# Gate and up projections in pairs: another buffer for half a weight set of the first pair, and another order of loads

## The chip, the cores and the metric

The kernel runs on one NeuronCore of a Trainium2 chip. Its engines are TensorE (matrix products; the profile's PE for matmuls, PEld for the weight loads beside them), VectorE (DVE), ScalarE (ACT), GpSimd (POOL) and SyncE (SP); each works through its own instructions in its own order. SP and POOL also issue the DMA transfers, each on a queue of its own, and both queues share 16 DMA engines. The metric is device time of one execution in microseconds (us). The profile is one execution of the program, taken by the hardware profiler.

## The reference, cut to what matters

One layer of a hybrid encoder on a sequence of 512 tokens of 1024 channels in float32. Three token mixers in parallel come first and are merged and projected; then follows the part that the change touches, a gated feed-forward network of width 2816:

```python
h2 = rms_norm(x, norm_ffn[l])
act = jax.nn.silu(jnp.einsum('bsd,df->bsf', h2, w_ffn_gate[l])) * jnp.einsum('bsd,df->bsf', h2, w_ffn_up[l])
x = x + jnp.einsum('bsf,fd->bsd', act, w_ffn_down[l])
```

## The kernel before

**Precision.** A float32 operand is split in two float32r parts: ScalarE rounds it to a high part, VectorE subtracts this from the operand and gives the low part (`split_a`, L1546 to 1554). A product is then three matmuls (high by high, high by low, low by high). The split weights lie in tags `whi` and `wlo` with 3 buffers each, so that splits run at most about two sets ahead of TensorE.

**The columns of the feed-forward network.** The 2816 columns are 11 chunks of 256. The first two (`NDIRECT`) are computed directly: `chan_chunk` for gate and up, `direct_act` for the activation (L1705 to 1721). The next six are taken as three pairs of chunks, u = 0, 1, 2 (`NTOK`, `seven_tok`, L1633), and the last three one by one, u = 3, 4, 5 (`seven`, L1587). Both of the latter compute gate and up together, by a scheme of seven products instead of eight: the operands are a 2 x 2 matrix of weight blocks (row: gate or up; column: first or second half of the 1024 input channels) and the normed input in blocks B. The seven weight operands of a pair, in the order of use (`ORDER`, L175), are

- 11, 12: blocks as loaded (gate, first and second half of the channels);
- S2 = 11 + 21 + 22 with the sign convention of the loaded blocks, S1 = 21 + 22, S3 = 11 + 21, S4 = S2 + 12;
- 22: as loaded (up, second half).

For a pair (u < 3) each weight set comes in two halves i = 0, 1 of 512 KB (128 partitions x 1024 values), written here 12_0, 12_1 and so on; S3_0, say, is the first half of S3. Each half is 12 matmuls of 512 columns (L1677). Products 11, S2 and S3 go to PSUM tile `ps_yh`, 12 to `ps_xl`, S1 and S4 to `ps_xh`, 22 to `ps_yl`.

**How the sets are made.** `make_a` (L1515) goes through `steps` (pair, set, half) some sets ahead of TensorE, and at each step loads, adds and splits what the step needs:

- `load_a(u)` (L1491) loads the sets that are built by accumulation. For pair 0: 21 (then 22 is added onto it by an accumulating DMA from POOL, giving S1) and 11 under the name S3 (then 21 is added by POOL, giving S3). For pairs 1 and 2: 11 and 21 (22 added by POOL, L1503). The loads are issued by SP (L1501). All of them lie in `corner` buffers.
- `load_raw(u, nm)` (L1505) loads 11, 12 and 22 by SP (L1509) into tag `raw` of pool `wp` (3 buffers). One half is an exception: 12_1 of pair 0 lies in a `g4` buffer.
- `make_s2` (L1511, VectorE at L1513) adds 21 and 11 to S2 in a `g4` buffer; L1542 adds 12 to it after S2 has been split, giving S4. For pairs 1 and 2, L1540 adds 21 onto 11 by a POOL DMA, giving S3, after 11 has been split.

**Buffers.** `corner` is a pool of 8 buffers of 4 KB a partition (L1270). Ahead of pair 0 they hold the 8 normed blocks and their differences (`hn`, `hnT`; L1444 and L1456); `split_b` (L1449) splits these for the seven products, and each buffer is free once all readers of its block are done. `g4` is a pool of 27 such buffers (`GBUFS`).

**When pair 1's loads are written.** L1519 calls `load_a` one pair ahead. While make_a is at 11, 12 or S2 of pair 0 only `load_a(0)` has been called; at S1 of pair 0 `load_a(1)` is. The order in which the instructions of an engine are finally issued is set by a planner (the Tile scheduler) from priorities, buffers and its own model of the times, and not by the order of the code alone; `tc.issue_after(ins)` adds an edge behind one instruction of the same engine. `make_a(3)` at L1709 is the first call, beside the direct chunk 1; it reaches 12_0 of pair 0.

Of the kernel before, what the change touches and what calls it, by code (L numbers as in the profile page):

```python
# [65 lines left out]
def layer_kernel(ctx: ExitStack, tc: tile.TileContext, x, xt, vecs, w_in, w_qkv7, w_gate7, w_pool, w_rg, w_ig,  # L66
                 w_branch, w_br7, w_out, w_fg, w_fu, w_fgu7, w_fgl7, w_fd, w_fd7, out):
    nc = tc.nc
# [51 lines left out]
    def two2(ap):  # L120
        if ap.shape[-1] == H:
            return ap.rearrange("p w (a b) -> p w a b", a=2)
        return ap.rearrange("p w (c a b) -> p (w c) a b", c=2, a=2)
# [163 lines left out]
    state = {"i": 1, "stop": n_before_down, "many": True}  # L287
# [150 lines left out]
    with ExitStack() as first:  # L438
# [477 lines left out]
        for cc in range(2):  # L916
# [14 lines left out]
            for nm in ORDER:  # L931
                ps, half, first_, t, ts_, src, ss = plan[nm]
# [39 lines left out]
    with ExitStack() as mix:  # L972
# [299 lines left out]
        def corner(shape, name, dt=F32):  # L1272

            return cor.tile([P] + shape, dt, tag="r", name=name)
# [91 lines left out]
    with ExitStack() as ffn:  # L1366
        gp = ffn.enter_context(tc.tile_pool(name="gp", bufs=GBUFS))

        def g4(shape, name, dt=F32):

            return gp.tile([P] + shape, dt, tag="g", name=name)
# [13 lines left out]
        for c in range(4):  # L1385
# [10 lines left out]
            for j in range(2):  # L1396
# [3 lines left out]
                t = x1p[c // 2, j][:, c % 2, :]  # L1400
# [81 lines left out]
        NU = DOWN - NDIRECT - NTOK  # L1482
        steps = [(u, nm, i) for u in range(NU) for nm in ORDER for i in range(2 if u < NTOK else 1)]
        raw = {}
        A = {}
        made = [0, 0]

        def usrc(u, nm, i):
            return w_fgu7[u, CH[nm], KH[nm], i]

        def load_a(u):  # L1491
            if u >= NTOK:
                for nm in ("11", "21", "22", "12"):
                    raw[u, nm, 0] = t = corner([2, 4, P], f"w{u}_{nm}")
                    nc.sync.dma_start(t, w_fgl7[u - NTOK, CH[nm], KH[nm]])
                return
            for nm, base, more in ((("21", "21", "22"), ("S3", "11", "21")) if u == 0
                                   else (("11", "11", None), ("21", "21", "22"))):
                for i in range(2):
                    raw[u, nm, i] = t = corner([2, 512], f"w{u}_{nm}{i}")  # L1500
                    nc.sync.dma_start(t, usrc(u, base, i))  # L1501
                    if more:
                        nc.gpsimd.dma_start(t, usrc(u, more, i), accum_op=ALU.add)  # L1503

        def load_raw(u, nm):  # L1505
            for i in range(2):
                raw[u, nm, i] = t = (g4([2, 512], f"w{u}_{nm}{i}") if (u, nm, i) == (0, "12", 1) else
                                     wp.tile([P, 2, 512], F32, tag="raw", name=f"w{u}_{nm}{i}"))
                nc.sync.dma_start(t, usrc(u, nm, i))  # L1509

        def make_s2(u, i):  # L1511
            raw[u, "S2", i] = t = g4([2, 512], f"w{u}_S2{i}")
            dve.tensor_tensor(t, raw[u, "21", i], raw[u, "11", i], ALU.add)  # L1513

        def make_a(upto):  # L1515
            while made[0] < min(upto, len(steps)):
                u, nm, i = steps[made[0]]
                made[0] += 1
                while made[1] < min(u + (1 if (u, nm) in ((0, "11"), (0, "12"), (0, "S2")) else 2), NU):  # L1519
                    load_a(made[1])  # L1520
                    made[1] += 1
                if u >= NTOK:
                    for s_, x, y, op in SUMS.get(nm, ()):
                        raw[u, s_, 0] = t = wp.tile([P, 2, 4, P], F32, tag="raw", name=f"w{u}_{s_}")
                        dve.tensor_tensor(t, raw[u, x, 0], raw[u, y, 0], op)
                    A[u, nm, i] = split_a(raw[u, nm, 0], f"{u}_{nm}")
                    continue
                if (nm, i) == ("11", 0):
                    if u == 0:
                        load_raw(u, "11")  # L1530
                    load_raw(u, "12")
                src = raw[u, nm if (u, nm) == (0, "S3") else FROM.get(nm, nm), i]
                A[u, nm, i] = split_a(src, f"{u}_{nm}{i}", (2, 512))
                if (u, nm, i) == (0, "12", 0):
                    with tc.issue_after(state["lo"]):
                        make_s2(u, 0)
                        make_s2(u, 1)
                if u and nm == "11":
                    make_s2(u, i)
                    nc.gpsimd.dma_start(raw[u, "11", i], usrc(u, "21", i), accum_op=ALU.add)  # L1540
                elif nm == "S2":
                    dve.tensor_tensor(src, src, raw[u, "12", i], ALU.add)  # L1542
                    if i:
                        load_raw(u, "22")

        def split_a(src, n, shape=(2, 4, P)):  # L1546
            if len(shape) == 2:
                h, l = (t.rearrange("p (k c) -> p k c", k=shape[0]) for t in weight_tiles("wh" + n, "wl" + n))
            else:
                h, l = (t.rearrange("p (w k c) -> p w k c", w=2, k=4)  # L1550
                        for t in weight_tiles("wh" + n, "wl" + n))
            act(h, src, AF.Copy)  # L1552
            state["lo"] = dve.tensor_tensor(l, src, h.bitcast(F32), ALU.subtract).ins  # L1553
            return h, l
# [32 lines left out]
        def seven(c):  # L1587
# [14 lines left out]
            for n, (nm, ps, half, first, t, ts_, src, ss) in enumerate(plan):  # L1602
                make_a(n0 + n + 3)
                product(A.pop((u, nm, 0)), B[0, WITH[nm]], ps, half, first, True)
                if t is not None:
                    last = act(two2(t[:, :, ts_]), in_order2(src[:, :, ss]), AF.Copy).ins
                if c == DOWN - 1 and nm in PRE:
                    split_d2("11", PRE.index(nm), 0, 0)
                if nm == "S4":
                    finish_act(tx, X, a[:, 0, :], 1.0)  # L1610
                if nm == "22":
                    finish_act(ty, Y, a[:, 1, :], -1.0)
                if tail and nm in ("11", "S2"):
                    tail.pop(0)()
                if toload and nm in LOADS.get(u - NTOK, ()):
                    with tc.issue_after(last):
                        load_act()
# [15 lines left out]
        def seven_tok(u):  # L1633
# [30 lines left out]
            for n, nm in enumerate(ORDER):  # L1664
# [4 lines left out]
                for i in range(2):  # L1669
                    make_a(n0 + 2 * n + i + 3)  # L1670
                    ah, al = A.pop((u, nm, i))
                    for a in range(2):
                        ts_ = slice(a * P, (a + 1) * P)
                        for kk in range(2):
                            k = 2 * i + kk
                            for m, (b_, a_) in enumerate(((bh, ah), (bh, al), (bl, ah))):
                                nc.tensor.matmul(ps[dst][:, a, :], b_[:, k, ts_], il(a_[:, kk, :]),  # L1677
                                                 start=dst == nm and m == k == 0, stop=m == 2 and k == 3,
                                                 skip_group_check=True)
# [25 lines left out]
        for c in range(NDIRECT):  # L1705
            pg = chan_chunk(("fg", c), h2, 3, fp)
            pu = chan_chunk(("fu", c), h2, 3, fp)
            if c == NDIRECT - 1:
                make_a(3)  # L1709
            a = g4([2, S], f"act{c}")  # L1710

            def direct_act(j, c=c, a=a, pg=pg, pu=pu):
                sg = small(f"sg{c}{j}", 2, "sq2")
                dve.tensor_tensor(two(sg), in_order(pg[j]), two(rb2), ALU.mult)
                act(sg, sg, AF.Silu)
                dve.tensor_tensor(two(sg), two(sg), in_order(pu[j]), ALU.mult)
                dve.tensor_tensor(a[:, j, :], sg, rb2, ALU.mult)

            if c < NDIRECT - 1:
                direct_act(0), direct_act(1)  # L1720
            acts[c] = a
# [15 lines left out]
        for m in range(4):  # L1737
            t = fp.tile([P, 2, S], F32, tag="mm", name=f"ps_d{m}")
# [121 lines left out]
        for nm in DORDER:  # L1860
# [3 lines left out]
            for q in range(2):  # L1864
                if (nm, q) == ("22", 1):

                    make_d(len(dsets))
                    for w, ps in enumerate((XY[1, "y"], XY[0, "x"])):
# [3 lines left out]
                        t = two2(x1p[q, 1][:, ws, lo])  # L1872
# [73 lines left out]
```

## Time and profile before

| what | value |
|---|---|
| median of 3 runs | 864.75 us (863.7 to 864.76) |
| the profiled execution | 863.47 us, of it 861.7 us span |
| mean granted TensorE clock | 0.996 |
| TensorE's share, 599.1 to 698 us | busy throughout |
| VectorE busy, 599.1 to 625 us | 20.17 of 25.9 us |
| VectorE busy, 625 to 661 us | 29.96 of 36 us |
| VectorE busy, 698 to 754 us | 52.98 of 56 us |

How to read the lines that follow below: a timeline row has the start in us from the start of the span, the duration, the engine, the line of the kernel, the operation, output and inputs, and in brackets the idle time of the engine before it with what ended that. SPq and POOLq are the engines' sequencers, which issue DMAs; the duration of an issue is not that of its transfer. A row of waits has who waited for whom, the us in total, how many times, and the longest. A row of the chain of waits has start, duration and what the time went to. A row of DMA issues has the size and the time from issue to landing. In the profile the weight tiles of the feed-forward network are called `w`, those whose names carry an S `w_S`; their split parts `wh`, `wl`, `wh_S`, `wl_S`.

### The profile page before, as it was taken

Reading aid. Unit: us, or ns where it says so; the run is one execution under the profiler, and the core shown is the slowest. Engines: PE = TensorE matmul, PEld = TensorE weight load, DVE = VectorE, ACT = ScalarE, POOL = GpSimd, SP = SyncE. Lnnn points to the kernel's source line nnn. Section 1 sums busy time; section 2 is a strip of 40 time slices with the busy share of each in tenths; the row PEclk is TensorE's granted clock in tenths of the full one; section 3 lists DMA queues with packets and bytes.
Section 4 is the critical chain, followed back from the end, with each engine's and each line's share of the span. In section 5 each row is a group of like instructions: output and inputs, shape, how many; then the busy total and the mean of one; then the engine's idle time right before and its main releaser. Section 6 shows DMA issues by size and latency. Waiting matters only on the chain.

```text
span 861.7 us, 13247 instructions
## 1 busy us (share of the span) xinstructions
PE 848.9 (99%) x4979; PEld 764.6 (89%) x4979; DVE 723.9 (84%) x925; ACT 530.3 (62%) x845; POOL 108.1 (13%) x152
## 2 busy tenths in 40 slices
PE   9999999999999999999999999997999999999998
PEld 6888888888889988888889988885888899999998
DVE  7899898988897699868997875896788799999974
ACT  6554999657887566656565544463555655755642
POOL 1110002223224101000011100010111010121200
PEclk9999999999999999999999999998999999999999
DMA  9686356798584768756668854279778737897913
GB/s 340 167 290 205 100 170 197 207 323 253 148 269 122 231 155 252 218 149 157 201 161 216 181 198 157 84 224 278 197 191 215 199 119 184 237 241 197 194 34 122
DMA packets 136897, 167.66 MB, mean 195 GB/s; under 512 B 66305, under 2 KB 103169, under 8 KB 136833
## 3 DMA queue, kind: packets, MB, share of 16 engines
q1 hardware_dynamic: 121472, 111.49, 41.8%
q0 software_dynamic: 15216, 55.06, 27.6%
q8 instruction: 39, 0.64, 0.3%
q14 instruction: 26, 0.20, 0.1%
q10 hardware_dynamic: 144, 0.26, 0.1%
HBM read 143.19 MB, written 22.02 MB: 192 GB/s over the span
## 4 chain that ended last, share of the span: by engine, by line
PE 75%; issue 8%; DVE 7%; ACT 4%; DMA 4%; POOL 1%; SPq 0%; POOLq 0%; DVEq 0%; ACTq 0%
PE ps_dy L1856 6%; PE ps_q L845 5%; PE ps_dx L1856 5%; PE ps_yh L1677 5%; PE ps_y L316 4%; PE ps_xh L1677 4%; PE ps_br L308 3%; PE ps_br L309 3%; PE ps_br L307 3%; PE ps_x L316 3%; PE ps_bY L1348 2%; PE ps_gy L316 2%; PE ps_gate L737 2%; DMA w<-in_w_ffn_dram 2%; DVE wlo L143 2%
## 5 line engine op out<-in xcount | busy, mean ns | idle before, releaser
L142 ACT ACTIVATE whi<-raw 128x1024 fp32r<-128x1024 f32 x69 | 72.9, 1056 | 72.2 <-PE ps_br L308 18.8
L143 DVE TENSOR_TENSOR wlo<-raw,whi 128x1024 fp32r<-128x1024 f32 x69 | 84.2, 1220 | 21.2 <-ACT whi L142 20.7
L143 DVE TENSOR_TENSOR wlo<-qw,whi 128x1024 fp32r<-128x1024 f32 x48 | 58.3, 1220 | 11.6 <-ACT whi L142 11.2
L142 ACT ACTIVATE whi<-qw 128x1024 fp32r<-128x1024 f32 x48 | 50.5, 1053 | 23.6 <-PE ps_q L845 14.3
L1552 ACT ACTIVATE wh<-w 128x1024 fp32r<-128x1024 f32 x27 | 28.5, 1057 | 30.3 <-DMA w<-in_w_ffn_dram 9.5
L1553 DVE TENSOR_TENSOR wl_S<-w_S,wh_S 128x1024 fp32r<-128x1024 f32 x26 | 31.6, 1220 | 11.9 <-ACT wh_S L1552 11.9
L1553 DVE TENSOR_TENSOR wl<-w,wh 128x1024 fp32r<-128x1024 f32 x27 | 32.9, 1218 | 9.5 <-ACT wh L1552 9.5
L1552 ACT ACTIVATE wh_S<-w_S 128x1024 fp32r<-128x1024 f32 x26 | 27.3, 1055 | 14.0 <-PE ps_y L316 6.9
L1552 ACT ACTIVATE whdS<-dw 128x1024 fp32r<-128x1024 f32 x20 | 21.2, 1058 | 21.3 <-PE ps_dy L1856 10.6
L1156 DVE TENSOR_TENSOR_SCAN E<-K,ahead 128x512 f32<-128x512 f32 (+3 forms) x32 | 25.4, 814 | 4.8 <-ACT K L1152 4.8
L1553 DVE TENSOR_TENSOR wldS<-dw,whdS 128x1024 fp32r<-128x1024 f32 x20 | 24.3, 1221 | 5.5 <-ACT whdS L1552 5.5
L1762 POOL DMA_DIRECT2D dw<-in_w_down_dram x20 | 17.1, 869 | 88.1 <-DVE wldS L1553 29.8
L307 PE MATMUL ps_lru<-HH,whi 128*128 128x512 f32 x64 | 24.6, 384 | 0.0
L308 PE MATMUL ps_br<-yHL,whi 128*128 128x512 f32 x64 | 24.4, 381 | 0.2 <-DMA yHL<-ydl 0.2
L307 PE MATMUL ps_br<-yph,whi 128*128 128x512 f32 x64 | 24.4, 382 | 0.0
L307 PE MATMUL ps_gate<-HH,whi 128*128 128x512 f32 x64 | 24.4, 381 | 0.0
L308 PE MATMUL ps_br<-ypl,whi 128*128 128x512 f32 x64 | 24.3, 380 | 0.0
L307 PE MATMUL ps_pool<-HH,whi 128*128 128x512 f32 x64 | 24.3, 379 | 0.0
L307 PE MATMUL ps_br<-yHH,whi 128*128 128x512 f32 x64 | 24.3, 379 | 0.0
L308 PE MATMUL ps_lru<-HL,whi 128*128 128x512 f32 x64 | 24.3, 379 | 0.0
L309 PE MATMUL ps_lru<-HH,wlo 128*128 128x512 f32 x64 | 24.3, 379 | 0.0
L308 PE MATMUL ps_gate<-HL,whi 128*128 128x512 f32 x64 | 24.3, 379 | 0.0
(825 smaller groups left out, 3281.5 us busy)
## 6 DMA issues: line engine op xcount, KB each, us to landing
raw<-in_w_in_dram SPq DMA_DIRECT2D x31, 512.0 KB, 4.7
qw<-in_w_qkv_dram SPq DMA_DIRECT2D x24, 512.0 KB, 6.7
w<-in_w_ffn_dram SPq DMA_DIRECT2D x24, 512.0 KB, 4.3
dw<-in_w_down_dram POOLq DMA_DIRECT2D x20, 512.0 KB, 7.7
raw<-in_w_branch_dram SPq DMA_DIRECT2D x16, 512.0 KB, 3.8
qw<-in_w_qkv_dram POOLq DMA_DIRECT2D x12, 512.0 KB, 8.4
g<-gd SPq DMA_DIRECT2D x24, 256.0 KB, 5.4
w<-in_w_ffnl_dram SPq DMA_DIRECT2D x12, 512.0 KB, 4.8
```

The costliest lines, as they stand in the source:

```text
L142: act(hi, raw, AF.Copy)
L143: los.append(dve.tensor_tensor(lo, raw, hi.bitcast(F32), ALU.subtract).ins)
L307: nc.tensor.matmul(ps, lh, rh, start=start, stop=False, skip_group_check=skip)
L308: nc.tensor.matmul(ps, lh, rl, start=False, stop=False, skip_group_check=skip)
L309: nc.tensor.matmul(ps, ll, rh, start=False, stop=stop, skip_group_check=skip)
L316: nc.tensor.matmul(o, a_[a][:, w, k, :], il2(b_[b][:, k, :]), start=first and n == k == 0, stop=last and n == 2 and k == 3, skip_group_che ...
L845: nc.tensor.matmul(ps[:, a, :], b_[:, k, ts_], il(a_[:, kk, :]), start=first and n == k == 0, stop=n == 2 and k == 3, skip_group_check=True)
L1156: dve.tensor_tensor_scan(E[:, c0:c0 + n][:, ::-1], K[:, c0 + 1:c0 + n + 1][:, ::-1], ahead[:, S - n:][:, ::-1], 0.0, ALU.mult, ALU.add)
L1552: act(h, src, AF.Copy)
L1553: state["lo"] = dve.tensor_tensor(l, src, h.bitcast(F32), ALU.subtract).ins
L1677: nc.tensor.matmul(ps[dst][:, a, :], b_[:, k, ts_], il(a_[:, kk, :]), start=dst == nm and m == k == 0, stop=m == 2 and k == 3, skip_group_ ...
L1856: nc.tensor.matmul(o, a_[a][:, w, k0 + k, :], il2(b_[b][:, k, :]), start=first and i == k == 0, stop=last and i == 2 and k == nk - 1, skip ...
```

## The change

Four things are done.

1. Half 12_1 of pair 0 is loaded into a `corner` buffer, no longer into a `g4` buffer.
2. For pair 0, the loads of 11 and 12 are written inside `load_a(0)`, between the loads of 21 and those of S3. Before, they were written after `load_a(0)`, at the step of 11.
3. `load_a(1)` is called one set later, at the step of S3 instead of S1 of pair 0, and the SP instructions it issues get an edge behind the last load that `load_raw` has written by then. That is 22_1 of pair 0, since the loads of 22 are written at the step of S2.
4. For pairs 1 and 2, `load_a` writes the loads of 21 ahead of those of 11; before, 11 came first.

```diff
-            for nm, base, more in ((("21", "21", "22"), ("S3", "11", "21")) if u == 0
-                                   else (("11", "11", None), ("21", "21", "22"))):
+            for nm, base, more in (("21", "21", "22"), ("S3", "11", "21") if u == 0 else ("11", "11", None)):
                 for i in range(2):
                     raw[u, nm, i] = t = corner([2, 512], f"w{u}_{nm}{i}")
                     nc.sync.dma_start(t, usrc(u, base, i))
                     if more:
                         nc.gpsimd.dma_start(t, usrc(u, more, i), accum_op=ALU.add)
+                if (u, nm) == (0, "21"):
+                    load_raw(u, "11")
+                    load_raw(u, "12")

         def load_raw(u, nm):
             for i in range(2):
-                raw[u, nm, i] = t = (g4([2, 512], f"w{u}_{nm}{i}") if (u, nm, i) == (0, "12", 1) else
+                raw[u, nm, i] = t = (corner([2, 512], f"w{u}_{nm}{i}") if (u, nm, i) == (0, "12", 1) else
                                      wp.tile([P, 2, 512], F32, tag="raw", name=f"w{u}_{nm}{i}"))
-                nc.sync.dma_start(t, usrc(u, nm, i))
+                state["raw"] = nc.sync.dma_start(t, usrc(u, nm, i)).ins
...
-                while made[1] < min(u + (1 if (u, nm) in ((0, "11"), (0, "12"), (0, "S2")) else 2), NU):
-                    load_a(made[1])
+                while made[1] < min(u + (1 if (u, nm) in ((0, "11"), (0, "12"), (0, "S2"), (0, "S1")) else 2), NU):
+                    with tc.issue_after(state["raw"]) if made[1] == 1 else nullcontext():
+                        load_a(made[1])
                     made[1] += 1
...
                 if (nm, i) == ("11", 0):
-                    if u == 0:
-                        load_raw(u, "11")
-                    load_raw(u, "12")
+                    if u:
+                        load_raw(u, "12")
```

## The prediction

> **What bounds the kernel now.** I read the page first, then TensorE's waits, its timeline around the one long wait, the chain that ended last, and then the SP queue and the landing of single loads there. 12_1 is the second half of pair 0's weight set 12, 1_21_0 the first half of pair 1's set 21, and so on.
>
> ```profile
> span 861.7 us, 13247 instructions
> PE 848.9 (99%) x4979; PEld 764.6 (89%) x4979; DVE 723.9 (84%) x925; ACT 530.3 (62%) x845; POOL 108.1 (13%) x152
> ...
> PE ps_xl L1677 <- ACT wh L1552: 5.2, 1, 5.2
> PE ps_xl L1677 <- DVE wl L1553: 0.5, 1, 0.5
> ```
>
> TensorE is busy for all but 12.8 us of the span. The last two rows are all its waits between 500 and 700 us, and they lie in one product, 12 of pair 0. From 599 us to the end the same view has no row: whatever TensorE gains ahead of 599 us reaches the end, unless the change makes a wait of its own. The stall, matmul by matmul, and the windows row behind it, whose last three figures are granted clock, DMA share and GB/s:
>
> ```profile
> 587.79 0.38 PE L1677 MATMUL ps_xl<-wl,B021h 128*128 128x512 f32 x1
> 588.00 0.38 PE L1677 MATMUL ps_xl<-wh,B021l 128*128 128x512 f32 x1
> 593.60 0.79 PE L1677 MATMUL ps_xl<-wh,B021h 128*128 128x512 f32 x1 [5.22 <-ACT wh L1552]
> 599.14 0.38 PE L1677 MATMUL ps_yh<-wh_S,B0T2h 128*128 128x512 f32 x1
> ...
> 593.60:599.10 5.50, 5.03 (x12) 3.75 (x13) 5.47 (x6) 2.75 (x3) 0.85 (x1) 0.55 1.06 241
> ```
>
> Matmuls follow each other at 588.00 - 587.79 = 0.215 us. The gap from 588.00 to 593.60 therefore loses 5.60 - 0.215 = 5.39 us. The 12 matmuls of 12_1 take 599.14 - 593.60 = 5.54 us where 12 x 0.215 = 2.58 would do, at a granted clock of 0.55: another 2.96. **The stall costs 8.35 us**, more than the 5.7 that the waits show. The chain of waits says what it waited for:
>
> ```profile
> 573.43 18.98 DMA w<-in_w_ffn_dram
> ...
> 592.49 1.06 ACT wh L1552
> ...
> 593.58 1.24 DVE wl L1553
> ```
>
> The load of 12_1 took 18.98 us. The SP queue's issues show why: start and duration, L1509 being the loads of 11, 12 and 22, L1501 the sets loaded ahead. The row at 569.70 is the second of the two at 567.41 alone, that at 598.47 the last of the three at 585.79. Below them stand the landing times in us of S3_0 (issued at 567.41), S3_1 (569.70), 12_0 (570.12) and 1_11_0 (570.78):
>
> ```profile
> 564.41 2.20 SPq L1501 DMA_DIRECT2D w<-in_w_ffn_dram  x2
> 567.41 2.62 SPq L1501 DMA_DIRECT2D w_S<-in_w_ffn_dram  x2
> 569.70 0.33 SPq L1501 DMA_DIRECT2D w_S<-in_w_ffn_dram  x1
> 570.12 0.38 SPq L1509 DMA_DIRECT2D w<-in_w_ffn_dram  x1
> 570.78 2.60 SPq L1501 DMA_DIRECT2D w<-in_w_ffn_dram  x3
> 573.43 0.70 SPq L1509 DMA_DIRECT2D w<-in_w_ffn_dram  x1
> 575.43 0.33 SPq L1501 DMA_DIRECT2D w<-in_w_ffn_dram  x1
> 585.79 13.01 SPq L1509 DMA_DIRECT2D w<-in_w_ffn_dram  x3
> 598.47 0.33 SPq L1509 DMA_DIRECT2D w<-in_w_ffn_dram  x1
> ...
> w_S<-in_w_ffn_dram SPq DMA_DIRECT2D x1, 512.0 KB, 4.5
> w_S<-in_w_ffn_dram SPq DMA_DIRECT2D x1, 512.0 KB, 8.7
> w<-in_w_ffn_dram SPq DMA_DIRECT2D x1, 512.0 KB, 12.1
> w<-in_w_ffn_dram SPq DMA_DIRECT2D x1, 512.0 KB, 15.2
> ```
>
> The order is 21_0, 21_1, S3_0, S3_1, 12_0, three loads of pair 1, whose products start only after all seven of pair 0's, then 12_1. They land in that order: 567.41 + 4.5 = 571.9, 569.70 + 8.7 = 578.4, 570.12 + 12.1 = 582.2, 570.78 + 15.2 = 586.0, and so on to 592.4. Three of pair 1's loads stand ahead of the one that TensorE waits for.
>
> **The change part by part.** (1) Pair 1's four loads go behind 22_1, the last load of pair 0. The second of the three L1509 issues in the 585.79 row is 22_1, near 587 (the additions of the 584.54 row further down free its buffer, by 586.9), so they come 12 to 16 us later and none is ahead of 12_1. (2) 12 is written ahead of S3, and 12_1 takes one of the eight corner buffers. These serve the normed blocks before, and they seem to be handed out as they come free:
>
> ```profile
> 566.13 1.22 DVE L1460 SCALAR_TENSOR_TENSOR hnT<-hnT,hn 128x1024 f32<-128x1024 f32 x1
> 567.26 1.22 DVE L143 TENSOR_TENSOR wlo<-raw,whi 128x1024 fp32r<-128x1024 f32 x1
> ```
>
> S3_0's issue at 567.41 follows the end of the first row, 567.35. That third buffer goes to 12_1; 12_0's buffer is freed by the second row at 568.48. So 12_0 and 12_1 can go at about 568.5 and 568.9, and 12_1 is fourth from 21_0 on, the place of S3_1: I take **578.4 for its landing**. Ends: 571.9 (S3_0's place) and 582.2 (12_0's, if one S3 load stays ahead). The deadline: its low part must be there for the second matmul, 588.43, and the chain puts 0.08 + 1.06 + 0.02 + 1.24 us between landing and that, so 586.0. Even the later end is 3.8 us early, and the DMA wait is gone.
>
> **What is late next** is VectorE's queue:
>
> ```profile
> 584.54 2.35 DVE L1513 TENSOR_TENSOR w_S<-w,w 128x1024 f32<-128x1024 f32 x2
> 600.59 1.22 DVE L1542 TENSOR_TENSOR w_S<-w_S,w 128x1024 f32<-128x1024 f32 x1
> 601.72 1.22 DVE L1553 TENSOR_TENSOR wl_S<-w,wh_S 128x1024 fp32r<-128x1024 f32 x1
> 604.49 5.18 PE ps_xh L1677 x24
> 609.66 5.18 PE ps_yh L1677 x24
> 620.02 5.18 PE ps_yl L1677 x24
> ```
>
> If its order stays, the two additions end at 586.9 and 12_1's low part at 588.1, 0.3 ahead of 588.43. From the start of that subtraction (593.58) to the end of S1_0's low part (602.94) VectorE runs almost without a pause, 9.36 us; begun at 586.9 it ends at 596.3, where S1's second matmul is due at 604.49 - 8.35 + 0.22 = 596.36. These margins are thin, so I charge **0.3 us** (bounds: 0, and 2.4 for two operations of 1.22 more in the way).
>
> (3) S3_0 and S3_1 move back two places, to land at 582.2 and 586.0, and each then takes an accumulation by POOL, whose order stays. Longest and shortest accumulation near there, and two loads, 1_12_0's at 598.47 (5.3) and 22_0's at 585.79 (9.2):
>
> ```profile
> w_S<-in_w_ffn_dram POOLq DMA_DIRECT2D x1, 512.0 KB, 12.9
> w<-in_w_ffn_dram POOLq DMA_DIRECT2D x1, 512.0 KB, 6.9
> w<-in_w_ffn_dram SPq DMA_DIRECT2D x1, 512.0 KB, 5.3
> w<-in_w_ffn_dram SPq DMA_DIRECT2D x1, 512.0 KB, 9.2
> ```
>
> S3_1 is complete at 592.9 to 598.9. Its second matmul is due at 609.66 - 8.35 + 2.59 + 0.22 = 604.1, less 2.4 for the split: 601.7. Nothing charged; 2.8 us of cover at the worse end.
>
> (4) Pair 1's loads now come as 21_0, 21_1, 11_0, 11_1 behind 22_1, from about 587.3 on, and are needed 8.35 us earlier than before. First come the additions for its S2:
>
> ```profile
> 614.52 1.22 DVE L1513 TENSOR_TENSOR w_S<-w,w 128x1024 f32<-128x1024 f32 x1
> 617.08 1.22 DVE L1553 TENSOR_TENSOR wl<-w,wh 128x1024 fp32r<-128x1024 f32 x1
> 618.21 1.22 DVE L1513 TENSOR_TENSOR w_S<-w,w 128x1024 f32<-128x1024 f32 x1
> ```
>
> The first is due at 614.52 - 8.35 = 606.2. 1_21_0 lands with 9.2 us at 596.5 and its accumulation with 6.9 (what this very accumulation took, issued at 591.69) at 603.4: 2.8 us spare, nothing charged. The bounds are 0 and the second rival. Counting S3 and 12_1 these are nine corner loads on eight buffers: the ninth, 1_11_1, waits for 12_1's buffer, last read by the second L1542 addition, which ends at 601.81 in the row above and 8.35 earlier in the new time, 593.5. It lands with 5.3 at 598.8 and has no accumulation; its reader is due at 618.21 - 8.35 = 609.9. Behind it on SP stands 1_12_0 (before at 598.47), whose product comes after pair 0's 22 and pair 1's 11, over 25 us later. (The Trainium skill, "DMA: Bandwidth & Descriptors", section "Anatomy of one DMA", says that a semaphore wait is spent on the issuing sequencer before dispatch, so this wait would hold every later SP load; by it the sum is unchanged as long as 1_12_0 is what stands behind. The SP view agrees that loads issue singly and late, with 13.01 us from the first to the end of the third of one L1509 row.)
>
> (5) The 27-buffer pool has one tile fewer; 12_1 was issued 0.05 us after its predecessor's issue ended (573.38), so it waited for no buffer there: 0.
>
> **Sum.** 863.47 (profiled execution; 861.7 of it span) - 8.35 + 0.3 = 855.4. The runs shown have a median 1.3 us above that execution, which gives 856.7; I name 856.0 between the two. (The Trainium skill, "TensorE: Matmul & The Clock Gate", Part 1, has the clock halved after an idle window of about 3.4 us and given back after as long of work. The trace agrees, with 0.55 behind a 5.4 us gap. By it a stall shorter than the window would cost no clock, and the sum stays.)
>
> **Rivals.** *Part of the stall stays* (0.23): two more VectorE operations ahead of a split cost 2.4 - 0.3 = 2.1 us; a 12.9 us accumulation of 1_21_0 stalls TensorE 1.3 us; an S3_1 accumulation as slow as 12_1's load (19.0) ends at 605.0, 3.3 late; with the 2.96 us of slow clock, 6.3. That is 857.2 to 861.4. For it: VectorE's margins of 0.1 to 0.3. Against: pair 1 does the same work at the same pace and TensorE never waits.
>
> *Pair 1 is fetched too late* (0.05, the slower side). If 1_21_0 takes 19.0 us like 12_1 before, and its accumulation 12.9, the sum lies at 587.3 + 31.9 = 619.2, 13.0 past the addition's due time. VectorE works in order, so the next low part, 22_0's (617.08 row, ending at 610.0 in new time, due at 620.02 - 8.35 + 0.22 = 611.9), has 1.9 to give. TensorE stalls 11.1 us, and 2.96 of slow clock with it: 863.47 - 8.35 + 14.1 = 869.2. It is slower than before by over 1.7 us from a stall of 7.1 us on, an accumulation that lands after 615.2. Against: 19.0 was paid with five loads unlanded ahead on the queue, and the change thins just that stretch.
>
> *The change doesn't do what it says* (0.09): the planner still puts 12_1 late, behind both S3 loads and in contention; then 863 to 865. Against: pair 1's loads are tied behind 22_1.
>
> **How the numbers follow.** Forecast 0.63 (855 to 857), rivals 0.23, 0.05, 0.09. The range takes the forecast and nearly all of the first rival, with 1 us below for the lower basis: 854.2 to 861.0. Faster by over 0.2% (1.7 us, about what a measurement of this kernel can tell from no change): 0.86; within: 0.09; slower: 0.05.
>
> **What would show it.** Right: no wait of the xl product for its high part, granted clock 1.00 from 580 to 600 us, 12_1 landing by 582, the S2 product starting near 591. Wrong: a VectorE low part as TensorE's new releaser in S2, S1 or S3 of pair 0 (the 0.3 was too small); POOL's accumulation as the releaser of VectorE near 606 to 612 (pair 1 too late); SP still issuing pair 1's loads ahead of 12_1.

## The result and the profile after

The changed kernel takes 856.84 us (median of 4 runs, 854.53 to 857.82), the kernel before beside it 864.49 us (4 runs, 863.7 to 864.76): a ratio of 0.9909 with a 95% interval of 0.9887 to 0.9931. The prediction was 856.0 us in a range of 854.2 to 861.0, faster with a chance of 0.86. The profiled execution of the changed kernel took 857.82 us, of it 856.0 us span, the longest of the four.

First the SP queue of the changed kernel. In the changed kernel L1511 issues 11, 12 and 22, L1500 the sets loaded ahead.

```profile
563.88 2.20 SPq L1500 DMA_DIRECT2D w<-in_w_ffn_dram  x2
567.97 0.80 SPq L1511 DMA_DIRECT2D w<-in_w_ffn_dram  x2
569.16 1.42 SPq L1500 DMA_DIRECT2D w_S<-in_w_ffn_dram  x2
584.82 1.46 SPq L1511 DMA_DIRECT2D w<-in_w_ffn_dram  x2
586.38 1.36 SPq L1500 DMA_DIRECT2D w<-in_w_ffn_dram  x3
590.68 0.33 SPq L1511 DMA_DIRECT2D w<-in_w_ffn_dram  x1
594.08 6.83 SPq L1500 DMA_DIRECT2D w<-in_w_ffn_dram  x5
```

The order is the one worked out: 21_0, 21_1, 12_0, 12_1, S3_0, S3_1, then 22_0 and 22_1, and only then three loads of pair 1. The ninth corner load, 1_11_1, waits until 594.08 for 12_1's buffer, and 1_12_0 even slips in ahead of it at 590.68. The load of 12_1 itself, the second issue of the 567.97 row (at 568.39), has this row of the DMA issues, with the time to landing last:

```profile
w<-in_w_ffn_dram SPq DMA_DIRECT2D x1, 512.0 KB, 6.8
```

It lands at 575.2, after 6.8 us in place of 18.98. TensorE, in the windows of the stall and behind it (the window's length, TensorE's busy time, and as the last three figures granted clock, DMA share and GB/s):

```profile
588.20:590.80 2.60, 2.60 (x14) 2.28 (x13) 2.57 (x4) 1.12 (x2) 0.00 (x0) 1.00 0.96 358
590.80:599.10 8.30, 8.30 (x40) 7.28 (x39) 6.72 (x6) 5.56 (x6) 1.70 (x2) 1.00 1.01 308
```

It is busy without a break and at full clock. In the chain of waits the products of pair 0 follow each other at 5.18 us:

```profile
580.08 5.18 PE ps_yh L1679 x24
585.26 5.18 PE ps_xl L1679 x24
590.44 5.18 PE ps_yh L1679 x24
595.62 5.18 PE ps_xh L1679 x24
```

Product S1 begins 604.49 - 595.62 = 8.87 us earlier than before. Of this 8.35 is the stall, the rest was there ahead of it: the first matmul of product 11 starts at 579.91 in this execution and at 580.45 in that of the kernel before. From that matmul to the first of S1 the timelines have 23.87 us before and 15.54 us now, a difference of 8.33.

Yet the two profiled executions are only 863.47 - 857.82 = 5.65 us apart. TensorE's waits over the whole span of the changed kernel say where the rest is:

```profile
PE ps_dx L1858 <- ACT whd L1554: 1.6, 1, 1.6
PE ps_q L845 <- DVE wlo L143: 1.5, 4, 0.5
PE warm_ps L452 <- DVE warm L329: 1.1, 1, 1.1
PE ps_dx L1858 <- DVE wld L1555: 0.8, 1, 0.8
```

The waits of `ps_xl` are gone, and 2.4 us of waits have come in the down projection, 200 us later. The chain has their cause and their end:

```profile
768.82 8.54 DMA dr<-in_w_down_dram
777.47 1.06 ACT whd L1554
778.56 1.23 DVE wld L1555
779.83 19.06 PE ps_dx L1858 x166
798.90 26.80 PE ps_dy L1858 x240
```

The kernel before has this row in its place:

```profile
804.56 26.80 PE ps_dy L1856 x240
```

The second `ps_dy` piece begins at 798.90, against 804.56 before: of 8.87 us there are 5.66 left. The 3.21 us that went are again more than the 2.4 us that the waits show. A load (`dr`) took 8.54 us there, 3.8 before. Whether that belongs to the change was the first question for the chip.

### The profile page after: what moved, and what is told of

Same layout as the page of the kernel before. It is cut to its first block, busy times and chain, and to the rows that moved or that the text cites. A ratio compares the mean times of both kernels' runs of the same rounds, so it can differ in the third digit from the quotient of the medians.

```text
span 856.0 us, 13245 instructions
## 1 busy us (share of the span) xinstructions
PE 846.4 (99%) x4979; PEld 763.6 (89%) x4979; DVE 723.5 (85%) x925; ACT 530.6 (62%) x845; POOL 108.1 (13%) x152
## 4 chain that ended last, share of the span: by engine, by line
PE 86%; DVE 5%; ACT 4%; issue 3%; DMA 1%; POOL 1%; SPq 0%; DVEq 0%; ACTq 0%; POOLq 0%
PE ps_yh L1679 5%; PE ps_q L845 5%; PE ps_dy L1858 5%; PE ps_dx L1858 4%; PE ps_y L316 4%; PE ps_xh L1679 4%; PE ps_br L308 3%; PE ps_br L307 3%; PE ps_br L309 3%; PE ps_x L316 3%; PE ps_bY L1348 3%; PE ps_gy L316 3%; PE ps_gate L737 2%; PE ps_bX L1348 2%; PE ps_gx L316 2%
```

## The experiments

The theory after the result: **only the time at which 12_1 lands counts, and that is set by what stands ahead of it on the SP queue.** The rivals: that the corner buffer, the order of 12 and S3, or the later loads of pair 1 are needed together; and that pair 1's loads slow 12_1 by contention wherever they stand.

**The changed kernel again**, unedited.

> The changed kernel, unedited, to look at its spread. Theory A: the whole stall of 8.35 us in product 12 of pair 0 goes in every execution, and the 2.4 us wait of TensorE in the down projection (product 12, ps_dx, for a dr load) that the first profile of the changed kernel shows comes and goes between executions: times from 854.5 to 858, and a second profile that shows less than 1.5 us of that wait in at least about half of the cases. Theory B: that wait belongs to the new order of loads and is there in every execution: every profile shows 2 us or more of it and every time is above 856.5.

Measured: 855.15 us (4 runs, 855.13 to 856.03), before 864.33 (7 runs); ratio 0.9898 (0.988 to 0.9916). Its profile has no wait in the down projection. This is POOL, first in the execution with the wait, then in this one, where POOL goes on to add 21 onto 11 of the down projection's weights:

```profile
748.01 0.85 POOL L1764 DMA_DIRECT2D dw<-in_w_down_dram  x1 [2.10 <-DVE wld L1555]
759.47 3.48 POOL L1764 DMA_DIRECT2D dw<-in_w_down_dram  x4 [10.60 <-DMA dw<-in_w_down_dram]
```

```profile
748.55 0.85 POOL L1764 DMA_DIRECT2D dw<-in_w_down_dram  x1 [1.45 <-DVE wld L1555]
754.24 1.73 POOL L1764 DMA_DIRECT2D dw<-in_w_down_dram  x2 [4.84 <-DMA dw<-in_w_down_dram]
```

In the one POOL stood 10.60 us for a load and then issued four accumulations at once, 9 us ahead of the `dr` load; in the other they were spread out. The expectation's theory A holds: the same program does both. The load that POOL stood for took 15.6 us in the one (issued at 743.31) and 9.8 us in the other (743.85). In the slow case one of POOL's accumulations was issued ahead of it, at 742.66, and in the other just behind it, at 743.86; whether that is the reason stays open.

**Only the later, tied loads of pair 1.**

```diff
 # kernel before
-                nc.sync.dma_start(t, usrc(u, nm, i))
+                state["raw"] = nc.sync.dma_start(t, usrc(u, nm, i)).ins
...
-                while made[1] < min(u + (1 if (u, nm) in ((0, "11"), (0, "12"), (0, "S2")) else 2), NU):
-                    load_a(made[1])
+                while made[1] < min(u + (1 if (u, nm) in ((0, "11"), (0, "12"), (0, "S2"), (0, "S1")) else 2), NU):
+                    with tc.issue_after(state["raw"]) if made[1] == 1 else nullcontext():
+                        load_a(made[1])
```

> The kernel before with only the call of load_a(1) one set later and its loads tied behind 22_1; 12_1 stays in g4, 12 stays behind S3. 12_1 is then sixth from 21_0 on (21_0, 21_1, S3_0, S3_1, 12_0, 12_1), the place that landed at 586.0 before. Theory (the place on the SP queue alone decides): landing 582 to 586, against a deadline of 586.0, so a TensorE wait of 0 to 1 us without loss of clock, 855.5 to 857.5. Rival (the buffer and the place ahead of S3 are needed): a wait of 3 us or more with a granted clock near 0.5 behind it, 859 or more.

**Only the order and the buffer.** Part 4, the order within pairs 1 and 2, stays in as well.

```diff
 # changed kernel
-                while made[1] < min(u + (1 if (u, nm) in ((0, "11"), (0, "12"), (0, "S2"), (0, "S1")) else 2), NU):
-                    with tc.issue_after(state["raw"]) if made[1] == 1 else nullcontext():
-                        load_a(made[1])
+                while made[1] < min(u + (1 if (u, nm) in ((0, "11"), (0, "12"), (0, "S2")) else 2), NU):
+                    load_a(made[1])
```

> The changed kernel with load_a(1) called at S1 again and without the tie: three loads of pair 1 go right behind S3_1, as in the kernel before, but 12_0 and 12_1 stand ahead of S3. Theory (the place on the queue alone decides): 12_1 lands at 574 to 579 as in the changed kernel, no stall, 855 to 857.5; S3_1 still lands at about 582 and the accumulation onto it later than in the changed kernel, without a TensorE wait. Rival (pair 1's loads take bandwidth from 12_1 though behind it): 12_1 lands after 584 and part of the stall stays, 858 or more.

**The changed kernel with the old buffer.**

```diff
 # changed kernel
-                raw[u, nm, i] = t = (corner([2, 512], f"w{u}_{nm}{i}") if (u, nm, i) == (0, "12", 1) else
+                raw[u, nm, i] = t = (g4([2, 512], f"w{u}_{nm}{i}") if (u, nm, i) == (0, "12", 1) else
```

> The changed kernel with 12_1 back in a g4 buffer, all else as changed; 12_1 then stands behind both S3 loads again, sixth from 21_0 on. Theory (place decides; the buffer only as far as it sets the place): landing 581 to 586, before the deadline of 586.0 or within 1 us of it, 855.5 to 857.5. Rival (the corner buffer itself brings the gain): the stall stays in part, 859 or more.

**Only the buffer.**

```diff
 # kernel before
-                raw[u, nm, i] = t = (g4([2, 512], f"w{u}_{nm}{i}") if (u, nm, i) == (0, "12", 1) else
+                raw[u, nm, i] = t = (corner([2, 512], f"w{u}_{nm}{i}") if (u, nm, i) == (0, "12", 1) else
```

> The kernel before with 12_1 in a corner buffer and nothing else changed. The planner then puts 12_1 directly behind 12_0, sixth from 21_0 on and ahead of pair 1's loads, which stay where they were. Theory (the place alone decides, however it comes about): landing 582 to 586.5, no TensorE wait or under 1 us, 855 to 857. Rival (the tie of pair 1's loads or 12 ahead of S3 is needed): a wait of 2 us or more, 858 and above.

All four have the whole gain: 856.16, 855.16, 855.27 and 855.45 us, ratios 0.9905 (0.9889 to 0.9921), 0.99 (0.9881 to 0.9918), 0.99 (0.9884 to 0.9917) and 0.9908 (0.9892 to 0.9924). None has a TensorE wait in the gate and up projections. So the later loads of pair 1 alone do it, order and buffer alone do it, and even the buffer alone does it, because the planner then issues 12_1 directly behind 12_0. In the last, pair 1's three loads follow on 12_1, and in the run with order and buffer they come right behind S3; 12_1 is in time in both, so loads of pair 1 behind it don't bring the stall back. What they do slow is POOL's accumulations onto S3, 8.5 and 9.2 us in the run with order and buffer against 5.9 and 5.4 us in the changed kernel, and TensorE doesn't wait for that. How near some of them come to the edge shows in ScalarE's split of 12_1, in the run with only the later loads and in the one with only the buffer:

```profile
587.03 1.06 ACT L1553 ACTIVATE wh<-w 128x1024 fp32r<-128x1024 f32 x1 [2.61 <-DMA w<-in_w_ffn_dram]
```

```profile
586.31 1.07 ACT L1552 ACTIVATE wh<-w 128x1024 fp32r<-128x1024 f32 x1 [2.75 <-DMA w<-in_w_ffn_dram]
```

In both ScalarE stood idle for this load and TensorE's waits show nothing. But with only the buffer TensorE's matmuls are at the edge, and two of product 12 start 0.29 us apart in place of 0.215:

```profile
588.72 0.46 PE L1677 MATMUL ps_xl<-wl,B021h 128*128 128x512 f32 x1
589.01 0.38 PE L1677 MATMUL ps_xl<-wh,B021l 128*128 128x512 f32 x1
```

**One, and two, loads of pair 1 ahead of 12_1** in place of three, to see the loss grow. The diff is that for one; for two, `>= 1` is `>= 2`.

```diff
 # kernel before
-                    nc.sync.dma_start(t, usrc(u, base, i))
+                    with tc.issue_after(state["raw", 0, "12"]) if u == 1 and 2 * (nm == "21") + i >= 1 else nullcontext():
+                        nc.sync.dma_start(t, usrc(u, base, i))
...
-                nc.sync.dma_start(t, usrc(u, nm, i))
+                state["raw", u, nm] = nc.sync.dma_start(t, usrc(u, nm, i)).ins
```

> The kernel before, with all of pair 1's loads but 1_11_0 tied behind 12_1, so that 12_1 has one load of pair 1 ahead of it in place of three: seventh from 21_0 on, the place that landed at 589.9 before. Theory (every place ahead of 12_1 delays it by what one load takes, and TensorE waits from 586.0 on): landing 589 to 590.5, a TensorE wait of 3 to 4.5 us; the clock may or may not fall for it. Without a fall the time is 858.1 to 859.6, with one like that of the kernel before (2.96 us) up to 862.6. Rival (the loss does not follow the place, it comes with contention from pair 1 as a whole): as before, a wait of 5 us or more, 863 and above.

> As the run with one load ahead, but with two (1_11_0 and 1_11_1) ahead of 12_1: eighth from 21_0 on, the place that landed at 591.15 before. Theory: landing 590.5 to 592, a TensorE wait of 4.5 to 5.5 us, the clock near 0.55 behind it, 861.5 to 863.5. Rival (contention as a whole): the same as with one load ahead.

Measured: 859.86 us (10 runs, 858.81 to 864.45) and 862.35 (10 runs, 858.55 to 863.47), before 863.77 (18 runs); ratios 0.9967 (0.9951 to 0.9984) and 0.9984 (0.9972 to 0.9997). TensorE's waits with one load ahead, and then with two:

```profile
PE ps_xl L1678 <- ACT wh L1553: 2.4, 1, 2.4
...
PE ps_xl L1678 <- DVE wl L1554: 0.8, 1, 0.8
```

```profile
PE ps_xl L1678 <- ACT wh L1553: 3.7, 1, 3.7
...
PE ps_xl L1678 <- DVE wl L1554: 0.5, 1, 0.5
```

3.2 and 4.2 us, as the places said (3 to 4.5 and 4.5 to 5.5; the latter a little less). By the timelines TensorE comes to S1 3.70 and 6.98 us later, counted from product 11 as in the section on the result, where the kernel before has 8.33. With the kernel before (5.7 us of waits) and those without a wait this makes a row. The landing is told from the start of product 11's first matmul in the same execution, to take out what differs ahead of it; the prediction's deadline of 586.0 is 586.0 - 580.45 = +5.6 on that scale.

| kernel | place of 12_1 from 21_0 on | it lands at | product 11 starts | difference | TensorE's wait | median, us |
|---|---|---|---|---|---|---|
| changed, again | 4 | 575.5 | 580.45 | -5.0 | none | 855.15 |
| order and buffer | 4 | 574.6 | 580.69 | -6.1 | none | 855.16 |
| changed, old buffer | 6 | 582.0 | 580.51 | +1.5 | none | 855.27 |
| later loads only | 6 | 587.0 | 581.97 | +5.0 | none | 856.16 |
| buffer only | 6 | 586.2 | 580.73 | +5.5 | none | 855.45 |
| one load ahead | 7 | 589.2 | 580.05 | +9.1 | 3.2 | 859.86 |
| two loads ahead | 8 | 591.0 | 580.60 | +10.4 | 4.2 | 862.35 |
| before | 9 | 592.4 | 580.45 | +12.0 | 5.7 | 863.77 |

The wait begins near +5.5 and then grows by about what the landing does (1.0 us of wait on 1.3 of landing, 1.5 on 1.6).

The place is not the whole of it: the sixth place lands at +1.5 where 12_0 is the third load and S3_0 the fourth, and at +5.5 where both halves of S3 come ahead of 12. Most of that is there two loads earlier. The fourth load and POOL's first accumulation (onto 21_0), with the old buffer and then with only the buffer:

```profile
568.99 0.38 SPq L1500 DMA_DIRECT2D w_S<-in_w_ffn_dram  x1
569.55 0.85 POOL L1502 DMA_DIRECT2D w<-in_w_ffn_dram  x1 [81.65 <-ACT B0T3h L1451]
```

```profile
569.99 0.33 SPq L1501 DMA_DIRECT2D w_S<-in_w_ffn_dram  x1
569.75 0.85 POOL L1503 DMA_DIRECT2D w<-in_w_ffn_dram  x1 [81.53 <-ACT B0T3h L1451]
```

In the first the fourth load goes out ahead of that accumulation and lands at 574.9, in the second it goes out behind it and lands at 578.6. All eleven profiles of this case fall in these two kinds. With the fourth load ahead of POOL's first accumulation (six profiles) the sixth load, whichever it is, lands at +1.5 to +2.8; with it behind (five) at +5.0 to +5.6. The order of 12 and S3 always went with it, so no run shows which of the two does it.

The clock answers less evenly than the wait. The windows behind the wait, with one load ahead and with two (clock third from the end):

```profile
592.00:594.00 2.00, 2.00 (x11) 1.76 (x10) 1.97 (x4) 1.13 (x2) 1.24 (x2) 1.00 0.96 365
```

```profile
593.00:598.00 5.00, 4.54 (x13) 3.64 (x13) 4.97 (x6) 1.98 (x3) 1.57 (x2) 0.55 0.98 232
```

After 3.2 us of waits the profiled execution kept the full clock and took 858.81 us; after 4.2 us it lost half of it and took 863.03. Over all executions the mean granted clock of a run tells them apart: with one load ahead 4 of 10 have 0.999 or 1.000 (858.81 to 859.51 us), the other six 0.996 or 0.998 (859.67 to 864.45); with two, one has 1.000 (858.55 us) and nine have 0.996 (862.08 to 863.47). The waits of the executions without a profile aren't known. With one load ahead the times lie 5.6 us apart, more than the 2.96 us that the slow clock cost before, so something besides the clock, perhaps the wait itself, differed between them.

**Pair 1 tied one step further**, behind 1_12_1: the slower rival's price.

```diff
 # changed kernel
+                    if made[1] == 1:
+                        load_raw(1, "12")
                     with tc.issue_after(state["raw"]) if made[1] == 1 else nullcontext():
                         load_a(made[1])
...
-                    if u:
+                    if u > 1:
                         load_raw(u, "12")
```

> The changed kernel with pair 1's loads tied one step further, behind 1_12_1, which waits for a buffer until about 609. This prices the slower rival, pair 1 fetched too late. Theory: 1_21_0 issues near 610, lands near 615, its accumulation near 622; VectorE's addition for S2 of pair 1 stands ahead of the low part of 1_11_0, so TensorE, due at 616.5 for product 11 of pair 1, starts it near 624.5: a wait of 6 to 9 us there and about 3 us of slow clock behind it, 864 to 868. Rival (later loads are absorbed, since sets are made ahead): under 2 us of wait, below 858.

Measured: 867.71 us (4 runs, 866.61 to 869.19), ratio 1.0045 (1.0027 to 1.0063). The chain of waits:

```profile
615.90 10.17 DMA w<-in_w_ffn_dram
...
626.09 0.04 DVE w_S L1515
626.13 1.11 issue
627.23 1.23 DVE wl L1557
628.46 0.04 issue
628.50 7.57 PE ps_yh L1681 x23
```

1_21_0's accumulation starts at 615.90 and lands at 626.07, VectorE's addition stands ahead of the low part of 1_11_0, and TensorE loses two waits of 7.5 and 3.0 us and 7.57 us for 23 matmuls that take 4.95 (0.215 each) at full clock. The mechanism is real and costs more than the first stall did; the wait is larger than expected (6 to 9) because the accumulation took 10.2 and not 6.9 us.

**The order within pair 1 undone** (11 ahead of 21 in `load_a` again, as in the kernel before).

```diff
 # changed kernel
-            for nm, base, more in (("21", "21", "22"), ("S3", "11", "21") if u == 0 else ("11", "11", None)):
+            for nm, base, more in ((("21", "21", "22"), ("S3", "11", "21")) if u == 0
+                                   else (("11", "11", None), ("21", "21", "22"))):
```

> The changed kernel with pairs 1 and 2 loading 11 ahead of 21 again. The ninth corner load is then 1_21_1, which waits for 12_1's buffer until about 594, lands near 600, and whose accumulation lands near 607 to 609; its reader, VectorE's second addition for S2 of pair 1, is due at 609.9. Theory (the order within pair 1 has nothing to do with the gain, and its own margin is thin but positive): no TensorE wait in pair 1, 855 to 856.5. Rival (21 has to come first, or VectorE waits for the accumulation and holds up the low parts of 22): a TensorE wait of 1 us or more between 605 and 620 us, 856.5 to 859.

Measured: 855.75 us (4 runs, 855.45 to 856.18), before 863.0 (7 runs), both on another chip than the runs above; ratio 0.9912 (0.9896 to 0.9929), and no TensorE wait there. The two additions of VectorE for pair 1's S2:

```profile
607.50 1.23 DVE L1516 TENSOR_TENSOR w_S<-w,w 128x1024 f32<-128x1024 f32 x1 [0.21 <-DMA w<-in_w_ffn_dram]
...
611.19 1.23 DVE L1516 TENSOR_TENSOR w_S<-w,w 128x1024 f32<-128x1024 f32 x1 [0.20 <-DMA w<-in_w_ffn_dram]
```

VectorE does wait for the accumulations, by 0.2 us each. The part brings nothing measurable, but in the order of the changed kernel that wait is not there.

## Why the prediction was right, step by step

- *The stall costs 8.35 us, not the 5.7 of the waits.* Shown. From profile to profile the kernel that again has no other new wait gives 863.47 - 855.16 = 8.31 us; the sum without its charge was 863.47 - 8.35 = 855.1, and the median of that set of runs is 855.15. From median to median the sets of runs without the stall give 7.65 to 9.18 us. A forecast from the waits alone would have said 857.8. That the forecast of 856.0 lies 0.84 us from the first median is in part luck: the sum without its charge is what the same program took the second time, and the first set had, in its profiled execution at least, a delay in the down projection that was in no term.
- *12_1 lands at 578.4.* It landed at 575.2, with product 11 starting 0.54 us earlier, so 2.7 us better. I gave it S3_1's place, whose load was issued at 569.70; 12_1 was out at 568.39, ahead of POOL's first accumulation (568.95), where S3_1's load had been behind it (569.19).
- *VectorE is next, 0.3 us.* Not needed. 12_1's low part, due at 588.43 - 0.54 = 587.89, ended 0.9 us early (first row below), and S1_0's, the first of the second row, at 595.16, with S1's second matmul due at 595.62 + 0.22:

```profile
585.80 1.22 DVE L1555 TENSOR_TENSOR wl<-w,wh 128x1024 fp32r<-128x1024 f32 x1
593.94 2.35 DVE L1555 TENSOR_TENSOR wl_S<-w,wh_S 128x1024 fp32r<-128x1024 f32 x2
```

- *S3 is late but covered.* Its second half landed at 581.8 where 586.0 was said. That is the sixth place's two landings again, and not the absence of pair 1's loads: with these right behind S3, in the run with order and buffer, it landed at 582.3. The accumulations took 5.9 and 5.4 us where 6.9 to 12.9 was said, and 8.5 and 9.2 us in the run with order and buffer.
- *Pair 1 stays in time.* Shown at both ends: 1_21_0's accumulation landed at 593.25 + 8.6 = 601.9, due at 606.2 (forecast 603.4); tied one step further it stalls TensorE, 867.71 us against the rival's 869.2.
- *What the prediction did not see.* It took the change's parts as one remedy. The buffer by itself and the later loads of pair 1 by themselves are each enough, since either has 12_1 issued ahead of pair 1; the order of 12 and S3 was run only together with one of them. The tie was given as what makes it sure, and it is not needed. And the scatter of 3.3 us between the changed kernel's first four runs was in no term: in the profiled execution a slow load in the down projection took 3.21 us back. That the other longer runs had the same cause wasn't seen, as they have no profile.

On the clock, the Trainium skill ("TensorE: Matmul & The Clock Gate", Part 1) has a free-running window of about 3.4 us, an idle one of which halves the clock. The profiles agree: behind the long waits of 5.2 us (before) and 3.7 us (two loads ahead) the clock was 0.55, and behind one of 2.4 us it stayed at 1.00. Over executions it is less clean: six of ten with one load ahead lost some clock, with waits that no profile recorded.

## What to carry to other kernels

When one load is late, list what stands ahead of it on its queue and ask of each when it is needed; a load that is ahead of its need (1_11_0 landed at 586.0 and was first read at 614.52) can cost a stall now, and moving it behind cost nothing here while it still met its own deadline. Price a stall of several us of TensorE by when its matmuls are back at full pace, not by the wait. And when a buffer is changed, look at the order that the planner then makes: here that alone moved the load.

## What was not expected of the hardware

Two loads in the same place on SP's queue landed 4.0 us apart (+1.5 and +5.5), as the fourth load went out ahead of POOL's first accumulation or behind it. While both queues were at work, accumulations (software_dynamic, POOL's) took far more of the DMA engines than plain loads (hardware_dynamic, SP's). The rows, with packets, MB and share of the 16 engines' time, are those of the run with only the buffer from 576 to 578 us:

```profile
q0 software_dynamic: 79, 0.27, 68.1%
q1 hardware_dynamic: 77, 0.29, 38.3%
```

By these rows a byte of an accumulation took nearly twice the engine time of a plain one (an estimate: 68.1 / 0.27 against 38.3 / 0.29). This suggests that accumulations on the other queue cost plain loads more than the loads behind them did, though no run changed the accumulations alone. And with one load of pair 1 ahead, the same program kept the full clock in four of ten executions and lost some of it in the others.
